# First block's attention: values by key tiles, later steps in the first pair, five early output tiles

## The chip, the cores and the metric

The kernel runs on one core of a Trainium2 chip. The core has TensorE (matrix products, with its own weight loads), VectorE, ScalarE and GpSimd (elementwise work), and SyncE, whose queue starts most DMAs. Each engine works through its own list of instructions in order and waits for others by semaphores. In the profile they are PE and PEld, DVE, ACT, POOL and SP. The metric is the device time of one execution in microseconds (us). Three runs of the kernel before took 1430.58, 1433.38 and 1433.93 us; the median is 1433.38.

## The reference

Two transformer blocks on 512 tokens of width 1024, in float32. The change touches the first one's mixer alone: attention of 16 heads of 64 with a forget gate, over 16 meta tokens and 512 real ones.

```python
def _fox_attend(q_blk, c_q, pos_q, k, v, c_k, pos_k):
    s = jnp.einsum('bhqd,bhkd->bhqk', q_blk, k).astype(jnp.float32) * (FOX_HEAD_DIM ** -0.5)
    s = s + (c_q[..., :, None] - c_k[..., None, :])
    s = jnp.where(pos_k[None, :] <= pos_q[:, None], s, -jnp.inf)
    p = jax.nn.softmax(s, axis=-1)
    return jnp.einsum('bhqk,bhkd->bhqd', p, v.astype(jnp.float32))

def fox_mixer(h, w_in, b_f, q_gain, k_gain, w_out):
    q, k, v, gate, f_logit = jnp.split(h @ w_in, [D, 2 * D, 3 * D, 4 * D], axis=-1)
    ...                                   # q, k: rms_norm over each head
    log_f = jax.nn.log_sigmoid(f_logit + b_f)
    c = jnp.cumsum(log_f, axis=1)
    ...                                   # _fox_attend in blocks of 128 queries
    o = o * jax.nn.sigmoid(gate)
    return o.astype(h.dtype) @ w_out
```

After it follow a gated feed-forward layer, and the second block with a chunked linear attention and a mixture of experts.

## The kernel before, in words

`fox` computes this mixer, and does two heads (a pair) at a time; there are eight pairs. All matrices are used in two parts, a rounded high one and the rest, so a product takes three matmuls per tile of 128 inputs.

**The order.** TensorE's main work is a list of projections, four per pair: queries (q), keys (k), values (v), gate (g). Each is made in eight parts (`project`, three matmuls of 512 columns per part, or six of 264). After each part `w.advance()` makes one step of a small planner (`Weave`): every piece of attention was put there with `at(delay, ...)`, counted in parts from the moment at which it was asked for. The delays are the table `F_V, Q_U, ...` at the head of the file. So the order of all instructions is fixed when the kernel is built, and pieces of one pair's attention stand between parts of the next pair's projections.

**The pieces.** `head_norm` takes a projection out of PSUM (L387), GpSimd makes its squares in two parts (`sqh` L391, `sql` L392), TensorE sums them over a head (L318, `sums`, due `Q_U` or `K_U` parts later), ScalarE and VectorE make the root of it (L220 to L228), VectorE scales (L401), and after `Q_H` or `K_H` parts the high and low copies for the scores are made (`hi`, `lo`; L428 to L450). For the first pair the forget gate's cumulated sum is made too (`forget_1` to `forget_3`, due `F_L`, and 2 and 4 parts after it).

`attend` puts down eight score blocks for the pair, four blocks of 128 queries for each of two heads (`scores`, every second part), each with its row maxima (L492), exponentials (L497) and scaling (L505). `F_F` parts after each comes `flip`: transposes of the probabilities on TensorE (L517) and their copy to `pt` by ScalarE (L519, the first five) or VectorE (L521). `values` (L529) multiplies them by the values, once per block of 128 queries, over the two to five key tiles that it sees: the blocks have 4, 6, 8 and 10 matmuls of 128 columns, the two heads in the two halves of the array's columns. `gated` and `gated_lo` then multiply by the gate into `ogh` and `ogl`.

In steady state the q sums stand three parts into the keys' projection, the k sums two parts into the values'. Three of the four `values` blocks stand ahead of the k sums.

**The end.** The output projection needs all pairs. So that TensorE has work during the last attention, three output tiles (`EARLY`) are computed without their last input tile first; then the planner is flushed, and the last input tile is added. The residual's input `h` is loaded by SP behind the weights that were asked for before. Transposes, sums and half a score block share the two PSUM slots `tp`; scores have `py`, projections `mm`.

Of the kernel before, what the change touches and what calls it, by code (L numbers as in the profile page):

```python
# [20 lines left out]
F32 = mybir.dt.float32  # L21
# [53 lines left out]

F_V, Q_U, Q_R, Q_H, Q_L, K_U, K_R, K_H, K_L, F_S, F_F, F_O, F_G, F_N, F_0, F_L = 6, 3, 2, 12, 1, 2, 2, 6, 2, 12, 8, 4, 12, 2, 5, 4

# [20 lines left out]
class Net:  # L98
# [142 lines left out]


    def fox(self):
        nc, tc, a = self.nc, self.tc, self.a
# [13 lines left out]

        fraw = wk.tile([P, KT, HEADS], F32, name="fraw")
        nc.scalar.dma_start(fraw, a["fw"])  # L260
# [21 lines left out]
        for i in range(NB):  # L282
            pt_off.append(pt_off[-1] + P * (i + 2))
        PW = pt_off[-1]
        pb = [sp.tile([P, PW], F32, name=f"pb{s}") for s in range(2)]
        for s in range(2):
# [7 lines left out]
        xl = sp.tile([P, KT, TM], F32R, name="xl")  # L294
        ss = sp.tile([P, TM], F32, name="ss")
        fhl = sp.tile([P, 2, KT, HEADS], F32R, name="fhl")
        self.split(fhl[:, 0], fhl[:, 1], fraw)
# [110 lines left out]
        def got_v(t, pv):  # L408
            v1 = wk.tile([P, TM], F32, name="v1", bufs=1)
            for p, o, n in pv:  # L410
                nc.vector.tensor_mul(v1[:, o:o + n], p, r1[:, o:o + n])

            def flip():
                vt = vts[t % 2]
                tp = pp.tile([P, T], F32, name="tp", bufs=2)
                for j in range(NB):
                    nc.tensor.transpose(tp[:, j * P:(j + 1) * P], v1[:, j * P:(j + 1) * P], self.ident)
                nc.scalar.activation(vt[:, 0:NB].rearrange("p j d -> p (j d)"), tp, AF.Copy)
                tp = pp.tile([P, T], F32, name="tp", bufs=2)
                nc.tensor.transpose(tp[:NM, :P], v1[:, T:TM], self.ident)  # L420
                nc.vector.tensor_copy(vt[:NM, NB], tp[:NM, :P])

            at(F_V, flip)

        def got_q(t, pq):
# [10 lines left out]

            head_norm(pq, self.qg, T, (hi, lo), Q_U, Q_R, Q_H, Q_L)

        def got_k(t, pk):
            def hi(kn):  # L440
                nc.scalar.activation(kd[A, 0], kn[A], AF.Copy)
                nc.scalar.activation(kd[B, 1], kn[B], AF.Copy)
                nc.scalar.dma_start(k2[HD:HD + 2, 0].bitcast(F32), nch[2 * t:2 * t + 1].bitcast(F32))
                nc.scalar.dma_start(k2[0:2, 1].bitcast(F32), nch[2 * t + 1:2 * t + 2].bitcast(F32))
                nc.scalar.activation(kd[B, 0], kn[A], AF.Copy)
                nc.scalar.activation(kd[A, 1], kn[B], AF.Copy)

# [3 lines left out]

            head_norm(pk, self.vec(V_KN), TM, (hi, lo), K_U, K_R, K_H, K_L)
            attend(t)
# [14 lines left out]
        def attend(t):  # L468
# [40 lines left out]
            def flip(i, s):  # L509
                if i == 0:  # L510
                    pts.append(wk.tile([P, PW], F32, name=f"pt{s}", bufs=1))
                for j0 in range(0, i + 2, 4):
                    n = min(4, i + 2 - j0) * P
                    c = pt_off[i] + j0 * P
                    tp = pp.tile([P, T], F32, name="tp", bufs=2)
                    for o in range(0, n, P):
                        nc.tensor.transpose(tp[:, o:o + P], pb[s][:, c + o:c + o + P], self.ident)  # L517
                    if F_E[2 * i + s]:
                        nc.scalar.activation(pts[s][:, c:c + n], tp[:, :n], AF.Copy)  # L519
                    else:  # L520
                        nc.vector.tensor_copy(pts[s][:, c:c + n], tp[:, :n])  # L521

            def values(i):
                if i == 0:
                    po.append(pp.tile([P, T], F32, name="plog", bufs=1))
                for j in range(i + 2):
                    c = pt_off[i] + j * P
                    for s in range(2):
                        nc.tensor.matmul(po[0][s * HD:(s + 1) * HD, i * P:(i + 1) * P],  # L529
                                         vt[:, j, s * HD:(s + 1) * HD], pts[s][:, c:c + P],  # L530
                                         start=(j == 0), stop=(j == i + 1), skip_group_check=True)

# [10 lines left out]
            for u in range(2 * NB):  # L543
                at(s0 + 2 * u, scores, u // 2, u % 2)
                at(s0 + F_F + 2 * u, flip, u // 2, u % 2)
            for i in range(NB):
                at(s0 + F_F + F_O + 4 * i + 2, values, i)
            at(s0 + F_F + F_O + 4 * NB, gated)
            at(s0 + F_F + F_O + 4 * NB + 2, gated_lo)

# [16 lines left out]
        self.w_at = 4 * PAIRS * KT  # L567
        EARLY = 3
        early = [mm() for _ in range(EARLY)]
        for p in early:  # L570
            for k in range(KT - 1):
# [14 lines left out]
        for m in range(KT):  # L586
            if m < EARLY:
                p = early[m]
# [973 lines left out]
def _layout(i):  # L1562
# [10 lines left out]
    wo = _tiles(f["fox_w_out"][0])  # L1573
    seq += [wo[:3, :7].reshape(-1, P, P), wo[:3, 7], *wo[3:]]
    wf, wo = _tiles(f["ffn_w_in"][0]), _tiles(f["ffn_w_out"][0])
# [53 lines left out]
```

## Time and profile before

| | |
|---|---|
| median of three runs | 1433.38 us |
| the profiled execution | 1431.87 us, span 1430.1 us |
| PE busy | 1355.8 us (95%), 8266 instructions |
| PEld busy | 1020.2 us (71%) |
| DVE, ACT, POOL busy | 739.3 (52%), 542.6 (38%), 118.9 us (8%) |

Busy shares are means over stages with different limits. The mixer takes about the first 340 us, and in it the engines other than PE are much busier than in the rest: in the page's 40 slices DVE shows 6 to 8 tenths in the first nine and 2 to 5 later. A row of the timeline gives the start, the time, the engine, the line, the operation, out<-in, the shape and how often; in brackets the engine's idle time before it, and what ended it. Rows of successive matmuls overlap, since each passes through a pipeline: their rate is read from their starts.

### The profile page before, as it was taken

How to read it: one execution, taken by the hardware profiler on the slowest of the kernel's cores; microseconds unless marked ns; L12 is line 12 of the kernel's file. 1: busy time of each engine (PE TensorE's matmuls, PEld its weight loads, DVE VectorE, ACT ScalarE, POOL GpSimd, SP SyncE). 2: the span in 40 equal slices, each digit the busy share in tenths (PEclk: the TensorE clock that was granted, in tenths of full speed). 3: DMA queues.
4: the chain of work that ended last, by engine and by line, in shares of the span. 5: the costliest groups of instructions: out<-in, count | busy, mean ns of one | idle time of the engine just before them, and what ended most of it. 6: DMA issues, size and time to landing. Idle time of an engine off the chain costs nothing.

```text
span 1430.1 us, 20194 instructions
## 1 busy us (share of the span) xinstructions
PE 1355.8 (95%) x8266; PEld 1020.2 (71%) x8266; DVE 739.3 (52%) x1321; ACT 542.6 (38%) x980; POOL 118.9 (8%) x111
## 2 busy tenths in 40 slices
PE   7899999999999999999999999999889999999995
PEld 5778888887888888888887888875556556556442
DVE  6778777785554433444456575542343432432333
ACT  6766776675433222323443444422111111111114
POOL 2101111111100000000322122000000000000001
PEclk9999999999999999999999999999989999999998
DMA  4111111113332222222221223698998999999995
GB/s 164 48 60 60 60 60 61 60 60 118 103 123 89 103 104 88 88 101 106 89 89 62 86 88 118 268 387 325 410 414 345 420 420 420 420 419 421 420 420 197
DMA packets 42495, 282.22 MB, mean 197 GB/s; under 512 B 4864, under 2 KB 5120, under 8 KB 9504
## 3 DMA queue, kind: packets, MB, share of 16 engines
q1 hardware_dynamic: 41616, 280.05, 49.3%
q8 instruction: 66, 1.08, 0.3%
q10 hardware_dynamic: 784, 0.85, 0.2%
q14 instruction: 29, 0.24, 0.0%
HBM read 278.72 MB, written 2.10 MB: 196 GB/s over the span
## 4 chain that ended last, share of the span: by engine, by line
PE 68%; DMA 19%; DVE 7%; ACT 3%; POOL 1%; issue 1%; SPq 0%; ACTq 0%; POOLq 0%; DVEq 0%
PE mm L205 22%; DMA wring<-in_w_dram 12%; PE mm L331 10%; PE py L205 8%; PE tp L205 8%; PE tp L1269 4%; PE mm L1359 3%; DMA v<-in_w_dram 3%; DMA wraw<-in_w_dram 3%; PE mm L773 2%; PE py L1303 2%; DMA whl<-in_w_dram 1%; PE plog L529 1%; POOL sql L392 1%; PE tp L517 1%; DVE whl L178 1%
## 5 line engine op out<-in xcount | busy, mean ns | idle before, releaser
L178 DVE TENSOR_TENSOR whl<-wraw,whl 128x1024 fp32r<-128x1024 f32 x138 | 180.8, 1310 | 100.2 <-ACT whl L168 100.0
L331 PE MATMUL mm<-xh,whl 128*128 128x264 f32 (+1 forms) x736 | 183.3, 333 | 2.2 <-ACT whl L168 2.1
L168 ACT ACTIVATE whl<-wraw 128x1024 fp32r<-128x1024 f32 x138 | 144.5, 1050 | 105.0 <-PE mm L205 44.3
L205 PE MATMUL mm<-xh,whl 128*128 128x512 f32 x544 | 175.9, 397 | 0.0
L331 PEld LDWEIGHTS mm<-xh,whl 128*128 128x128 f32 x736 | 120.6, 190 | 17.6 <-issue 3.4
L1269 PEld LDWEIGHTS tp<-h,xt 128*128 128x128 f32 x1024 | 115.9, 192 | 6.9 <-issue 2.5
L205 PEld LDWEIGHTS mm<-xh,whl 128*128 128x128 f32 x544 | 102.2, 188 | 23.1 <-issue 2.3
L1269 PE MATMUL tp<-h,xt 128*128 128x128 f32 x1024 | 118.4, 276 | 0.2 <-DVE h L1260 0.2
L205 PE MATMUL mm<-xl,whl 128*128 128x512 f32 x272 | 106.0, 390 | 0.0
L331 PE MATMUL mm<-xl,whl 128*128 128x264 f32 (+1 forms) x368 | 100.1, 325 | 0.0
L1359 PE MATMUL mm<-wring,h 128*32 128x512 f32 x664 | 96.1, 595 | 3.4 <-ACT h L1272 2.0
L1308 DVE SCALAR_TENSOR_TENSOR h<-py,sv,h 128x512 fp32r<-128x512 f32 (+1 forms) x33 | 24.1, 734 | 143.3 <-ACT h L1305 143.3
L205 PE MATMUL mm<-ogh,whl 128*128 128x512 f32 x256 | 83.6, 396 | 1.5 <-ACT ogh L536 1.5
L1272 ACT ACTIVATE h<-tp,vecs 128x128 f32<-128x128 f32 x128 | 36.5, 368 | 105.1 <-PE tp L1269 105.1
L1370 ACT ACTIVATE tmp<-mm,sv 128x256 f32<-128x256 f32 x16 | 7.6, 473 | 181.0 <-PE mm L1359 165.9
L1289 DVE TENSOR_TENSOR acc<-acc,mm 128x512 f32<-128x512 f32 (+1 forms) x120 | 73.8, 673 | 1.3 <-PE mm L1288 1.0
L1287 PE MATMUL mm<-h,ss 128*128 128x512 f32 (+1 forms) x128 | 61.8, 484 | 9.2 <-DVE acc L1289 5.1
L205 PE MATMUL py<-xh,whl 128*128 128x512 f32 x208 | 65.8, 391 | 0.0
L205 PE MATMUL tp<-xh,whl 128*128 128x512 f32 x208 | 65.2, 389 | 0.0
L331 PEld LDWEIGHTS mm<-xl,whl 128*128 128x128 f32 x368 | 62.2, 191 | 3.3
L616 POOL TENSOR_TENSOR ss<-ss,sq 128x512 f32<-128x512 f32 x21 | 29.1, 1401 | 403.0 <-ACT sq L612 403.0
L205 PEld LDWEIGHTS mm<-xl,whl 128*128 128x128 f32 x272 | 51.1, 188 | 11.5 <-issue 1.4
(420 smaller groups left out, 2539.2 us busy)
## 6 DMA issues: line engine op xcount, KB each, us to landing
wring<-in_w_dram SPq DMA_DIRECT2D x120, 1024.0 KB, 19.8
wraw<-in_wd_dram SPq DMA_DIRECT2D x69, 1024.0 KB, 4.8
whl<-in_w_dram SPq DMA_DIRECT2D x27, 1024.0 KB, 16.8
v<-in_w_dram SPq DMA_DIRECT2D x20, 1024.0 KB, 18.0
wraw<-in_w_dram SPq DMA_DIRECT2D x18, 1024.0 KB, 19.8
h<-in_xT_dram SPq DMA_DIRECT2D x8, 256.0 KB, 5.6
acc<-in_w_dram SPq DMA_DIRECT2D x2, 1024.0 KB
wring<-in_w_dram SPq DMA_DIRECT2D x4, 512.0 KB, 17.0
```

Source lines behind the costliest of these rows:

```text
L168: self.nc.scalar.activation(hl[:, 0], raw, AF.Copy)
L178: self.nc.vector.tensor_sub(hl[:, 1], raw, hl[:, 0].bitcast(F32))
L205: self.nc.tensor.matmul(out, w, x[:, first + k], start=(at + k == 0 and e == 0), stop=(at + k == of - 1 and e == 2))
L331: nc.tensor.matmul(p[:rows, :m], w[:, wi, k], xx[:, k, o:o + m], start=(n == 0), stop=(n == 3 * KT - 1))
L616: nc.gpsimd.tensor_add(ss, ss, sq)
L773: nc.tensor.matmul(pv[b], x[:, k, bs], w2[:, wi, k % 2], start=(k == 0 and e == 0), stop=(k == KT - 1 and e == 2))
L1269: nc.tensor.matmul(p[:, k], self.xt[:, b, (k0 + k) * P:(k0 + k + 1) * P], oh[:, 1, b], start=(b + k == 0), stop=(b == NB - 1), skip_group_ ...
L1272: nc.scalar.activation(xs[:, k0 + k], p[:, k], AF.Copy, scale=self.vec(V_FN2, k0 + k))
L1287: nc.tensor.matmul(pc, gt[:, b * P:(b + 1) * P], yh[:, hs], start=True, stop=False)
L1289: nc.vector.tensor_add(acc[b][:, hs], acc[b][:, hs] if q else self.xt[:, b, hs], pc)
L1303: nc.tensor.matmul(out, hT[:, e, js], w, start=(e == 0), stop=(e == 1))
L1359: nc.tensor.matmul(ps[32 * j:32 * j + 32], xs[:, kind * 4 + k, 32 * j:32 * j + 32], self.ring[kind, 4 * q + j][:, k * T:(k + 1) * T], star ...
```

## The change

1. `values` goes by key tiles: for each of the five key tiles and each head one matmul over all queries that see that tile (512, 512, 384, 256 and 128 columns), where it was one block of queries over its key tiles. `pt` is laid out by key tile for it, with `flip`'s copies writing up to four runs of 128. All of a pair's `values` now come after its last `flip`, from `F_O` parts on, one key tile per part; `gated` and `gated_lo` come 2 and 4 parts behind.
2. In the first pair the keys' steps come later (`K_0`), the flip of the values too (`F_V0`), the attention starts 9 instead of 5 parts later than in other pairs (`F_0`), the forget gate 6 instead of 4 (`F_L`); the second pair's query copies come at 14 instead of 12 (`Q_H1`).
3. `EARLY` is 5 instead of 3; the last two of these tiles take `py` slots.
4. In `got_k` all four key copies precede the two small DMAs into `k2`.
5. `fraw`, `ss` and `fhl` take buffers of names that are used later.

```diff
-F_V, Q_U, Q_R, Q_H, Q_L, K_U, K_R, K_H, K_L, F_S, F_F, F_O, F_G, F_N, F_0, F_L = 6, 3, 2, 12, 1, 2, 2, 6, 2, 12, 8, 4, 12, 2, 5, 4
+F_V, Q_U, Q_R, Q_H, Q_L, K_U, K_R, K_H, K_L, F_S, F_F, F_O, F_G, F_N, F_0, F_L = 6, 3, 2, 12, 1, 2, 2, 6, 2, 12, 8, 3, 12, 2, 9, 6
+
+F_V0, K_0, Q_H1 = 14, (9, 2, 13, 2), 14
...
-        fraw = wk.tile([P, KT, HEADS], F32, name="fraw")
+        fraw = wk.tile([P, KT, HEADS], F32, name="sqh", bufs=2)
...
-        ss = sp.tile([P, TM], F32, name="ss")
-        fhl = sp.tile([P, 2, KT, HEADS], F32R, name="fhl")
+        ss = wk.tile([P, TM], F32, name="sql", bufs=2)
+        fhl = wk.tile([P, 2, KT, HEADS], F32R, name="v1")
...
-            at(F_V, flip)
+            at(F_V if t else F_V0, flip)
...
-            head_norm(pq, self.qg, T, (hi, lo), Q_U, Q_R, Q_H, Q_L)
+            head_norm(pq, self.qg, T, (hi, lo), Q_U, Q_R, Q_H1 if t == 1 else Q_H, Q_L)
...
                 nc.scalar.activation(kd[B, 1], kn[B], AF.Copy)
+                nc.scalar.activation(kd[B, 0], kn[A], AF.Copy)
+                nc.scalar.activation(kd[A, 1], kn[B], AF.Copy)
                 nc.scalar.dma_start(k2[HD:HD + 2, 0].bitcast(F32), nch[2 * t:2 * t + 1].bitcast(F32))
                 nc.scalar.dma_start(k2[0:2, 1].bitcast(F32), nch[2 * t + 1:2 * t + 2].bitcast(F32))
-                nc.scalar.activation(kd[B, 0], kn[A], AF.Copy)
-                nc.scalar.activation(kd[A, 1], kn[B], AF.Copy)
...
-            head_norm(pk, self.vec(V_KN), TM, (hi, lo), K_U, K_R, K_H, K_L)
+            head_norm(pk, self.vec(V_KN), TM, (hi, lo), *((K_U, K_R, K_H, K_L) if t else K_0))
...
             def flip(i, s):
                 if i == 0:
-                    pts.append(wk.tile([P, PW], F32, name=f"pt{s}", bufs=1))
+                    pts.append(wk.tile([P, NB + 1, T], F32, name=f"pt{s}", bufs=1))
...
+                    dst = pts[s][:, j0:j0 + n, i * P:(i + 1) * P]
...
-            def values(i):
-                if i == 0:
+                        nc.vector.tensor_copy(dst, tp[:, :n])
+
+            def values(j):
+                if j == 0:
                     po.append(pp.tile([P, T], F32, name="plog", bufs=1))
-                for j in range(i + 2):
-                    c = pt_off[i] + j * P
-                    for s in range(2):
-                        nc.tensor.matmul(po[0][s * HD:(s + 1) * HD, i * P:(i + 1) * P],
-                                         vt[:, j, s * HD:(s + 1) * HD], pts[s][:, c:c + P],
-                                         start=(j == 0), stop=(j == i + 1), skip_group_check=True)
+                for s in range(2):
+                    nc.tensor.matmul(po[0][s * HD:(s + 1) * HD, first_q[j]:], vt[:, j, s * HD:(s + 1) * HD],
+                                     pts[s][:, j, first_q[j]:], start=(j == 0), stop=(j == NB),
+                                     skip_group_check=True)
...
-            for i in range(NB):
-                at(s0 + F_F + F_O + 4 * i + 2, values, i)
-            at(s0 + F_F + F_O + 4 * NB, gated)
-            at(s0 + F_F + F_O + 4 * NB + 2, gated_lo)
+            o0 = s0 + F_F + 4 * NB - 2 + F_O
+            for j in range(NB + 1):
+                at(o0 + j, values, j)
+            at(o0 + NB + 2, gated)
+            at(o0 + NB + 4, gated_lo)
...
-        EARLY = 3
-        early = [mm() for _ in range(EARLY)]
-        for p in early:
+        early = []
+        for n in range(self.EARLY):
+            p = mm() if n < 3 else f_bank()
+            early.append(p)
```

On TensorE, in the fifth pair's projections: the last rows of the fourth pair's attention and the fifth's keys' sums. `pb` are probabilities, `plog` the output of `values`, `sqh` and `sql` the squares. Before:

```order
L517 MATMUL tp<-ident,pb_129 128x128 x4
L529 MATMUL plog<-pt_1801,vt_139 64x128
L529 MATMUL plog<-pt_1821,vt_139 64x128
...
L331 MATMUL mm<-xh,whl 128x264 x2
L517 MATMUL tp<-ident,pb_129 128x128 x5
L529 MATMUL plog<-pt_1801,vt_139 64x128
L529 MATMUL plog<-pt_1821,vt_139 64x128
...
L318 MATMUL tp<-sqh,hones 128x264
L318 MATMUL tp<-sql,hones 128x264
```

And of the kernel after, the same place:

```order
L524 MATMUL tp<-ident,pb_129 128x128 x5
L325 MATMUL tp<-sqh,hones 128x264
L325 MATMUL tp<-sql,hones 128x264
...
L535 MATMUL plog<-pt_1747,vt_139 64x512
L535 MATMUL plog<-pt_1767,vt_139 64x512
L338 MATMUL mm<-xh,whl 128x264 x2
L338 MATMUL mm<-xl,whl 128x264 x2
L338 MATMUL mm<-xh,whl 128x264 x2
L535 MATMUL plog<-pt_1747,vt_139 64x512
L535 MATMUL plog<-pt_1767,vt_139 64x512
```

The `values` rows between and behind the transposes are gone from there; the keys' sums follow the last transposes at once, and all values come behind them, one key tile after each part.

On ScalarE, where the second pair's query and key copies stand (`qs`, `q` and `kd`, `k`), near the end of the first pair's probabilities. Before:

```order
L519 ACTIVATE pt_624<-tp 128x512
L428 ACTIVATE qs<-q_559 64x512
L429 ACTIVATE qs<-q_559 64x512
L430 ACTIVATE q_122<-q_559 64x512
L431 ACTIVATE q_122<-q_559 64x512
L441 ACTIVATE kd<-q_681 64x528
L442 ACTIVATE kd<-q_681 64x528
L443 DMA k_123<-nch 2x1x528
L444 DMA k_123<-nch 2x1x528
L445 ACTIVATE kd<-q_681 64x528
```

After:

```order
L435 ACTIVATE qs<-q_543 64x512
L436 ACTIVATE qs<-q_543 64x512
L437 ACTIVATE q_122<-q_543 64x512
L438 ACTIVATE q_122<-q_543 64x512
L448 ACTIVATE kd<-q_653 64x528
L449 ACTIVATE kd<-q_653 64x528
L450 ACTIVATE kd<-q_653 64x528
L451 ACTIVATE kd<-q_653 64x528
L452 DMA k_123<-nch 2x1x528
L453 DMA k_123<-nch 2x1x528
L527 ACTIVATE pt_662<-tp 128x4x128
```

The copy of the fifth transposed block to `pt` stood ahead of the query copies and now stands behind the key copies and the DMAs.

## Rows read from the trace of the kernel before

**Rows 1.** Windows, one pair: stretch, us, engines' busy time, PEclk, DMA share, GB/s.

```profile
173.45:189.90 16.45, 15.81 (x137) 14.10 (x136) 13.91 (x28) 11.67 (x24) 5.58 (x4) 1.00 0.05 9
189.90:210.18 20.28, 20.28 (x133) 16.95 (x132) 15.43 (x33) 14.13 (x30) 0.00 (x0) 1.00 0.26 98
```

**Rows 2.** Timeline of PE in these two stretches (start, us, what).

```profile
177.10 0.66 PE L529 MATMUL plog<-pt,vt 128*64 128x128 f32 x8
177.69 0.51 PE L331 MATMUL mm<-xh,whl 128*128 128x264 f32 x2
...
180.26 0.66 PE L517 MATMUL tp<-ident,pb 128*128 128x128 f32 x4 [0.38 <-ACT pb L497]
...
187.78 1.09 PE L529 MATMUL plog<-pt,vt 128*64 128x128 f32 x16
...
189.43 0.39 PE L318 MATMUL tp<-sql,hones 128*128 128x264 f32 x1
...
192.57 0.41 PE L331 MATMUL mm<-xh,whl 128*128 128x264 f32 x2
192.91 1.31 PE L529 MATMUL plog<-pt,vt 128*64 128x128 f32 x20
194.15 0.51 PE L331 MATMUL mm<-xh,whl 128*128 128x264 f32 x2
```

**Rows 3.** Timeline of DVE in the first of the two.

```profile
173.65 0.69 DVE L387 TENSOR_TENSOR q<-mm,r 128x512 f32<-128x512 f32 x1 [0.28 <-PE mm L331]
...
175.59 1.48 DVE L505 TENSOR_SCALAR pb<-pb,mx 128x400 f32<-128x400 f32 x1
...
178.47 0.41 DVE L492 TENSOR_REDUCE mx<-tp 128x1 f32<-128x264 f32 x1
...
180.81 0.69 DVE L222 TENSOR_SCALAR rs_x<-tp 128x512 f32<-128x512 f32 x1 [0.94 <-ACT rr L220]
...
185.21 0.77 DVE L387 TENSOR_TENSOR q<-mm,r 128x264 f32<-128x264 f32 x2
```

**Rows 4.** Timeline of ACT there.

```profile
179.64 0.47 ACT L497 ACTIVATE pb<-tp,mx 128x264 f32<-128x264 f32 x1
```

**Rows 5.** Timeline of POOL there.

```profile
187.21 2.17 POOL L392 TENSOR_TENSOR sql<-sq,sqh 128x528 fp32r<-128x528 f32 x1
```

**Rows 6.** Timeline of PE in the experts' stage, four column groups.

```profile
1204.25 0.60 PE L1359 MATMUL mm<-whl,h 128*32 128x512 f32 x3
...
1204.67 0.60 PE L1359 MATMUL mm<-whl,h 128*32 128x512 f32 x3
```

**Rows 7.** Waits of PE, 26 to 80 us: who for whom, us in total, times, longest.

```profile
PE tp L417 <- DVE v L411: 3.1, 1, 3.1
PE tp L318 <- POOL sql L392: 2.1, 2, 1.1
PE tp L318 <- ACT pb L497: 1.6, 1, 1.6
```

**Rows 8.** Windows in the first pair.

```profile
46.50:52.00 5.50, 5.47 (x16) 4.38 (x17) 3.38 (x5) 2.45 (x5) 0.00 (x0) 0.50 0.01 2
70.00:76.00 6.00, 4.12 (x36) 3.51 (x34) 4.18 (x9) 4.64 (x14) 1.33 (x1) 1.00 0.33 112
```

**Rows 9.** Timeline of PE in the first pair.

```profile
36.38 0.39 PE L318 MATMUL tp<-sql,hones 128*128 128x264 f32 x1 [0.99 <-POOL sql L392]
```

**Rows 10.** Timeline of ACT in the first pair.

```profile
50.48 0.64 ACT L445 ACTIVATE kd<-q 64x528 fp32r<-64x528 f32 x1 [3.01 <-DVE k L450]
51.13 0.64 ACT L446 ACTIVATE kd<-q 64x528 fp32r<-64x528 f32 x1
```

**Rows 11.** Timeline of PE at the mixer's end.

```profile
339.25 0.50 PE L205 MATMUL mm<-ogh,whl 128*128 128x512 f32 x1 [1.48 <-ACT ogh L536]
...
339.98 0.50 PE L205 MATMUL mm<-ogl,whl 128*128 128x512 f32 x1 [0.22 <-DVE ogl L540]
```

**Rows 12.** The page's part 6, DMA issues: count, KB each, us to landing.

```profile
wraw<-in_wd_dram SPq DMA_DIRECT2D x69, 1024.0 KB, 4.8
```

More of the change, by code (lines that the diff above doesn't have):

```diff
@@ L240, in split @@
             nc.vector.scalar_tensor_tensor(lo, src, scale, hi.bitcast(F32), op0=OP.mult, op1=OP.subtract)
+    EARLY = 5
     def fox(self):
@@ L284, in fox @@
         PW = pt_off[-1]
+        first_q = [max(j - 1, 0) * P for j in range(NB + 1)]
         pb = [sp.tile([P, PW], F32, name=f"pb{s}") for s in range(2)]
@@ L510, in flip @@
                 if i == 0:
-                    pts.append(wk.tile([P, PW], F32, name=f"pt{s}", bufs=1))
+                    pts.append(wk.tile([P, NB + 1, T], F32, name=f"pt{s}", bufs=1))
                 for j0 in range(0, i + 2, 4):
-                    n = min(4, i + 2 - j0) * P
+                    n = min(4, i + 2 - j0)
                     c = pt_off[i] + j0 * P
-                    tp = pp.tile([P, T], F32, name="tp", bufs=2)
-                    for o in range(0, n, P):
-                        nc.tensor.transpose(tp[:, o:o + P], pb[s][:, c + o:c + o + P], self.ident)
+                    tp = pp.tile([P, 4, P], F32, name="tp", bufs=2)
+                    for o in range(n):
+                        nc.tensor.transpose(tp[:, o], pb[s][:, c + o * P:c + (o + 1) * P], self.ident)
+                    dst = pts[s][:, j0:j0 + n, i * P:(i + 1) * P]
                     if F_E[2 * i + s]:
-                        nc.scalar.activation(pts[s][:, c:c + n], tp[:, :n], AF.Copy)
+                        nc.scalar.activation(dst, tp[:, :n], AF.Copy)
                     else:
-                        nc.vector.tensor_copy(pts[s][:, c:c + n], tp[:, :n])
-            def values(i):
-                if i == 0:
+                        nc.vector.tensor_copy(dst, tp[:, :n])
+            def values(j):
+                if j == 0:
                     po.append(pp.tile([P, T], F32, name="plog", bufs=1))
-                for j in range(i + 2):
-                    c = pt_off[i] + j * P
-                    for s in range(2):
-                        nc.tensor.matmul(po[0][s * HD:(s + 1) * HD, i * P:(i + 1) * P],
-                                         vt[:, j, s * HD:(s + 1) * HD], pts[s][:, c:c + P],
-                                         start=(j == 0), stop=(j == i + 1), skip_group_check=True)
+                for s in range(2):
+                    nc.tensor.matmul(po[0][s * HD:(s + 1) * HD, first_q[j]:], vt[:, j, s * HD:(s + 1) * HD],
+                                     pts[s][:, j, first_q[j]:], start=(j == 0), stop=(j == NB),
+                                     skip_group_check=True)
             def gated():
@@ L586, in fox @@
         for m in range(KT):
-            if m < EARLY:
+            if m < self.EARLY:
                 p = early[m]
@@ L1573, in _layout @@
     wo = _tiles(f["fox_w_out"][0])
-    seq += [wo[:3, :7].reshape(-1, P, P), wo[:3, 7], *wo[3:]]
+    e = Net.EARLY
+    seq += [wo[:e, :7].reshape(-1, P, P), wo[:e, 7], *wo[e:]]
     wf, wo = _tiles(f["ffn_w_in"][0]), _tiles(f["ffn_w_out"][0])
```

## The prediction

> **What bounds the kernel now.** The change touches only the first block's attention, about the first 340 of 1430 us, so I read the windows of one pair of heads first, then each engine's timeline in it. In steady state a pair takes 36.73 us, and it falls into two stretches of different kind [rows 1]. Stretch A, 16.45 us, runs from the end of the next pair's query projection to the sums of squares of its keys; there TensorE has holes. In stretch B, 20.28 us, TensorE is busy for all 20.28 us: it sets the pace alone. The reader is to see this contrast, because the change moves TensorE work from A to B.
>
> What sets the pace in A? I followed it through the other engines [rows 2 to 5]. The queries' end lets VectorE start at 173.65. Its scaling of a probability block then takes 1.48 us; the maxima of the eighth score block come only at 178.47, though TensorE had left those scores before 177.10. ScalarE's exponential of them runs at 179.64, the logarithm for the queries comes behind it, VectorE waits for that until 180.81 and reaches the keys' scaling at 185.21. GpSimd's second square pass starts at 187.21 and takes 2.17 us, and TensorE starts the last sums at 189.43. Nowhere in this chain does an engine wait for a values matmul. TensorE's transposes at 180.26 themselves wait for ScalarE [rows 2]. So A is a chain of VectorE, ScalarE and GpSimd, into whose waits three of the four values blocks (8, 12 and 16 records at 177.10, at 182.75 by the same pattern, and at 187.78) are put as filler. The fourth, at 192.91, lies in B.
>
> **The change, part by part.**
>
> *Values by key tiles.* Columns first: before, 28 matmuls of 128 columns; after, 10 of 512, 512, 384, 256 and 128 (two heads each). Both are 3584, so nothing is saved in streaming. The records show two per matmul. From the starts of the 8-record block and its successor (0.59 us) and of the 20-record block and its successor (1.24 us) [rows 2], a record costs (1.24 - 0.59) / 12 = 0.054 us. The block at 192.91 follows two matmuls begun at 192.57; 528 columns at 2.4 GHz are 0.22 us, so the block costs 194.15 - 192.79 = 1.36 us, of which 20 x 0.054 = 1.08 is streaming and 0.28 is the price of entering and leaving. Are 512 columns run beside each other as well as 128? No such two-head matmul is in this trace; the nearest is the expert stage, where four column groups of 512 columns take 0.42 us per four records [rows 6], which is two passes of 512 columns at 2.4 GHz for all four at once. I take the same rate. All five blocks then cost 56 x 0.054 + 5 x 0.28 = 4.43 us, where the four cost 3.03 + 1.12 = 4.15. The bounds are 3.03 (no block price) and 7.5 (the two heads one after the other).
>
> The Trainium skill, in TensorEngine Tiling (Array Packing), section Instruction Overhead, speaks against this: each matmul has an overhead of about 60 cycles, so 36 fewer records would save an estimated 36 x 25 ns = 0.9 us a pair. The records' 0.054 us for 128 columns leaves no room for it (128 columns at 2.4 GHz are 0.053). By the rule each of eight pairs would take 0.9 us less, and the sum below would come to about 1442.
>
> *Their place.* The rows in the order of TensorE show that all five blocks now stand behind the last sums of the keys, in B. A loses 36 x 0.054 + 3 x 0.28 = 2.79 us of TensorE work. If the chain sets A, A stays at 16.45 us: I followed it above, and the order of VectorE's instructions in A is unchanged. B, which TensorE sets, gets 4.43 - 1.36 = 3.07 us more. So **a pair takes 3.07 us longer**; if A shrank by the whole 2.79, it would be 0.28. I take 3.07, the row-by-row chain. It holds for the attention of pairs 1 to 6, which lies beside projections of pairs 2 to 7: 6 x 3.07 = 18.4 us. For the first and the last pair I count the fifth block alone: 2 x 0.28 = 0.6 us. The gating and its two halves come later too; the projection behind them covers that, since nothing reads them before the output projection.
>
> *The first pair.* It removes waits of TensorE: 3.1 us for the values' scaling, 2.1 and 1.6 us among others [rows 7], and after the first of these 5.50 us at a granted clock of 0.50, 1.2 GHz [rows 8], of which half, 2.75 us, is lost. That is 9.5 us at best. It brings waits. (a) The keys' sums move from 36.38 [rows 9] to behind four parts of the gate, near 39.2 by counting the parts ahead at 0.70 to 0.73 us each (three matmuls of 512 columns, or six of 264, with the gaps between them); the copies of the keys ended 15.4 us after the sums, 3.0 of them blocked by the two small DMAs that now come behind them [rows 10]. With four query copies of about 0.64 us now ahead of the key copies, the first scores can start at about 39.2 + 15.4 - 3.0 + 4 x 0.64 = 54, or 1 us sooner, as the last copies serve the second head only: 53. TensorE has work, twelve more parts and the transposes of the values, until about 49, so it waits some 4 us, and again the clock may fall for 2.75 us. (b) ScalarE now copies the fifth of the eight transposed probability blocks (the order's second place) behind four query and four key copies, 8 x 0.64 = 5.1 us; two parts of projection, 1.4 us, and two pieces of attention cover some 2.1 of it, so about 3 us show in a later transpose that needs the slot. Removed 9.5, brought about 4 + 2.75 + 3 = 9.8: **I take 0**, with -9.5 (none of the new waits) and +5 (old ones at 60 to 75 us stay) as ends.
>
> *Five output tiles early.* The work is the same, 42 matmuls of 512 columns come earlier. They cover the last pair's gating, at which TensorE waits 1.48 + 0.22 = **1.7 us** now [rows 11]; that goes. What would be late next are the residual's loads, which stand behind one weight load more on SP's queue: that is hidden by 14 more steps of TensorE work; without the cover it is at most one weight load, 4.8 us [rows 12].
>
> *Buffers.* The forget weights and the sum of squares share buffers with later tiles; their readers are long done when those are first written: nothing either way. The key copies before the DMAs: later pairs reach their scores 3 us later, which covers it; at worst 2 x 0.64 us a pair.
>
> **Sum.** The profiled execution took 1431.87 us (span 1430.1), 1.5 below the median of the runs, which I do not add. 1431.87 + 18.4 + 0.6 + 0 - 1.7 = **1449.2 us**.
>
> **Rivals.**
> 1. *TensorE sets A after all* (not slower). If VectorE's chain would move up when TensorE arrives earlier, each pair pays 0.28: 1431.87 + 6 x 0.28 + 0.6 - 1.7 = 1432.5 us; with the first pair's best end it is 1423. For it: TensorE is 15.81 of 16.45 us busy in A. Against: 180.26 and 189.43 wait for ScalarE and GpSimd already. It decides where the keys' end at 185.21 moves up against the queries' end.
> 2. *The clock falls in the longer holes.* The wait of 0.38 us before 180.26 would grow by the first block's 0.7, the one before 189.43 by the third block's 1.1, in every pair. If that sends the clock to 0.50 as the 3.1 us wait did, six times 2.75 us come on top: about 1466 us. Against: the wait of 1.6 us in the first pair lies in a stretch at 1.00 [rows 8].
> 3. *The two heads' matmuls run one after the other at 512 columns*, so the change doesn't do what it says: 3.03 us more in eight pairs, 1449 + 24 = 1473 us. Against: [rows 6].
>
> **How the numbers follow.** Forecast 0.75, rival 1 0.15, rival 2 0.06, rival 3 0.04. The forecast's own range, by the first pair's ends, is 1439 to 1455. The range is 1432 to 1460: it leaves out the lower part of rival 1 and rivals 2 and 3. About 0.3%, 4.3 us, can be told from no change. Slower: forecast, rivals 2 and 3, less what the first pair's best end and an error of mine in the chain could take: 0.80. No change: most of rival 1 and a little of the forecast, 0.13. Faster: rival 1 with a good first pair, 0.07.
>
> **What would show it.** Right: a pair's period near 39.8 us; from the queries' end to the keys' sums still about 16.4, with TensorE's busy time there down by some 2.8; a wait of TensorE for GpSimd's second square pass longer by about 1.1 us in every pair; B near 23.4 and fully busy; a block of four 512-column records about 0.87 us plus 0.28; no wait for the gating at the end. Wrong: a period near 37 us (rival 1), a granted clock below 1.00 between 90 and 310 us (rival 2), blocks of 1.7 us (rival 3), or first scores of the first pair well before 53 us.

## Result and profile after

| | runs | median | lowest to highest |
|---|---|---|---|
| before | 4 | 1432.37 us | 1430.58 to 1433.93 |
| after | 4 | 1453.77 us | 1452.15 to 1456.64 |

The table has one more run of the kernel before (1431.36 us) than the three that were known ahead of the prediction. The ratio is 1.0149, with a 95% interval of 1.0136 to 1.0162: the change makes the kernel 21.4 us slower. The profiled execution took 1456.64 us, the slowest of the four. Its page (its span, then each engine's busy time):

```profile
span 1454.9 us, 19626 instructions
...
PE 1367.5 (94%) x7978; PEld 1006.6 (69%) x7978; DVE 738.7 (51%) x1321; ACT 543.8 (37%) x980; POOL 119.8 (8%) x111
```

TensorE is busy 11.7 us longer though it runs 288 matmul records fewer (36 per pair), so some 13 us of the 24.8 us of span are idle time. Where? First the two stretches of one pair, as in [rows 1], here from the queries' end to the end of the keys' sums and from there to the next queries' end; columns are span, then PE, PEld, DVE, ACT, POOL, PEclk, DMA share, GB/s:

```profile
183.69:199.94 16.25, 13.60 (x101) 12.21 (x100) 13.82 (x28) 11.66 (x24) 5.58 (x4) 1.00 0.04 6
199.94:223.59 23.65, 23.65 (x134) 16.95 (x132) 15.54 (x33) 14.35 (x30) 0.00 (x0) 1.00 0.23 87
```

Stretch A is 16.25 us long against 16.45, though TensorE works 13.60 us in it instead of 15.81. Stretch B has become 23.65 us instead of 20.28, and TensorE is busy in all of it. The clock is 1.00 in both. So the reader sees 2.2 us of TensorE's work leave A, and A stay as it was.

TensorE's own timeline shows what took the place of the values in A, against [rows 2]:

```profile
190.49 0.66 PE L524 MATMUL tp<-ident,pb 128*128 128x128 f32 x4 [0.75 <-ACT pb L504]
...
195.39 0.33 PE L524 MATMUL tp<-ident,pb 128*128 128x128 f32 x1 [0.43 <-DVE pt L529]
...
198.99 0.36 PE L325 MATMUL tp<-sqh,hones 128*128 128x264 f32 x1 [1.10 <-DVE pt L529]
199.47 0.39 PE L325 MATMUL tp<-sql,hones 128*128 128x264 f32 x1
...
201.87 0.40 PE L338 MATMUL mm<-xh,whl 128*128 128x264 f32 x2
202.21 1.08 PE L535 MATMUL plog<-pt,vt 128*64 128x512 f32 x4
203.22 0.51 PE L338 MATMUL mm<-xh,whl 128*128 128x264 f32 x2
```

The wait for exponentials has grown from 0.38 to 0.75 us (190.49), a wait of 0.43 for a copy is new (195.39), and so is one of 1.10 before the keys' sums (198.99). A block of values is the row at 202.21. It lies between the end of the two matmuls begun at 201.87 (528 columns, 0.22 us) and 203.22, so it takes 1.13 us; [rows 2] had 1.36 for the largest of the old blocks.

The release at 198.99 is VectorE's. Its timeline:

```profile
196.72 1.52 DVE L180 TENSOR_TENSOR whl<-wraw,whl 128x1024 fp32r<-128x1024 f32 x1
198.16 0.88 DVE L529 COPY pt<-tp 128x512 f32<-128x512 f32 x2
```

Its last copies to `pt`, which free a slot `tp` for the sums, stand behind a weight split of 1.52 us. But they are not what ends A. The second sums start only at 199.47, 0.48 us behind the first, and this is 0.05 us after GpSimd's second square pass ends (197.24 + 2.18 = 199.42):

```profile
197.24 2.18 POOL L399 TENSOR_TENSOR sql<-sq,sqh 128x528 fp32r<-128x528 f32 x1
```

In the kernel before it was the same: that pass ends at 187.21 + 2.17 = 189.38, and the second sums start at 189.43 [rows 2, 5]. So in both traces A's end follows GpSimd's pass, and an earlier copy alone would not have brought the second sums forward; no run tried it.

How the difference adds up is read from GpSimd's first square pass of each pair's queries, which marks the start of a period. After (third, fourth and eighth pair):

```profile
104.26 1.04 POOL L398 TENSOR_TENSOR sqh<-q 128x512 fp32r<-128x512 f32 x1 [36.49 <-ACT ogh L542]
...
144.76 1.04 POOL L398 TENSOR_TENSOR sqh<-q 128x512 fp32r<-128x512 f32 x1 [25.14 <-DVE q L394]
...
304.34 1.04 POOL L398 TENSOR_TENSOR sqh<-q 128x512 fp32r<-128x512 f32 x1 [25.16 <-DVE q L394]
```

Before (third and eighth):

```profile
100.97 1.04 POOL L391 TENSOR_TENSOR sqh<-q 128x512 fp32r<-128x512 f32 x1 [29.53 <-DVE q L387]
...
284.67 1.04 POOL L391 TENSOR_TENSOR sqh<-q 128x512 fp32r<-128x512 f32 x1 [21.81 <-DVE q L387]
```

The third pair starts 104.26 - 100.97 = 3.29 us later. The eighth starts 304.34 - 284.67 = 19.67 later, so five periods cost 16.38, the first of them 3.8 and the others 3.15 each. A product of the feed-forward layer that stood at 391.78 stands at 414.02: 22.24 later, 2.57 more. The rest of this profile's 24.8 us is lost in the experts' stage (last section).

### The profile page after: what moved, and what is told of

The parts are those of the page before. It is cut to its first block, busy times and chain, and to the rows that moved or that the text cites. A ratio compares the mean times of both kernels' runs of the same rounds, so it can differ in the third digit from the quotient of the medians.

```text
span 1454.9 us, 19626 instructions
## 1 busy us (share of the span) xinstructions
PE 1367.5 (94%) x7978; PEld 1006.6 (69%) x7978; DVE 738.7 (51%) x1321; ACT 543.8 (37%) x980; POOL 119.8 (8%) x111
## 4 chain that ended last, share of the span: by engine, by line
PE 78%; DVE 7%; ACT 7%; DMA 3%; POOL 2%; issue 2%; ACTq 0%; SPq 0%; POOLq 0%; DVEq 0%
PE mm L207 19%; PE mm L338 8%; PE py L207 8%; PE tp L1277 7%; PE tp L207 7%; PE mm L1367 7%; PE py L1311 4%; DMA wring<-in_w_dram 3%; PE mm L781 2%; PE plog L535 2%; PE mm L1295 2%; PE tp L1288 2%; PE mm L1296 2%; POOL sql L399 1%; DVE whl L180 1%
## 5 line engine op out<-in xcount | busy, mean ns | idle before, releaser
L338 PE MATMUL mm<-xh,whl 128*128 128x264 f32 (+1 forms) x736 | 190.6, 337 | 2.4 <-ACT whl L170 1.5
L207 PE MATMUL mm<-ogh,whl 128*128 128x512 f32 x224 | 73.6, 395 | 0.0
## 6 DMA issues: line engine op xcount, KB each, us to landing
whl<-in_w_dram SPq DMA_DIRECT2D x27, 1024.0 KB, 11.7
```

Source lines behind the costliest of these rows:

```text
L207: self.nc.tensor.matmul(out, w, x[:, first + k], start=(at + k == 0 and e == 0), stop=(at + k == of - 1 and e == 2))
L338: nc.tensor.matmul(p[:rows, :m], w[:, wi, k], xx[:, k, o:o + m], start=(n == 0), stop=(n == 3 * KT - 1))
```

## Experiments

All times are against the kernel before on the same chip (1432.4 to 1433.3 us in the four sets). "A period" is the row of the stretch between two such square passes. The edits are shown in part: `...` marks lines left out, and the lines of the table of delays are shortened to the names that bear on the run.

**1. Values by key tiles alone.**

```diff
-F_O, F_0, F_L = 4, 5, 4
+F_O, F_0, F_L = 3, 5, 4
-            def values(i):
+            def values(j):
...
+            for j in range(NB + 1):
+                at(o0 + j, values, j)
```

> The kernel before with part 1 of the change alone: values by key tiles, all behind the pair's last transposes. My theory (TensorE work leaves a stretch that other engines pace and is put into one that TensorE paces): the period of a pair 36.73 becomes 39.9 us, as in the changed kernel, so 6 x 3.15 = 18.9 us for pairs 2 to 7, and some 3 us more where the first pair's values leave its holes too: about +20 to +22 us against the kernel before. Rival (the first pair's moved steps and the five early tiles carry a good part of the 21 us): under +15 us.

**2. The old blocks at the new place.**

```diff
-                at(s0 + F_F + F_O + 4 * i + 2, values, i)
-            at(s0 + F_F + F_O + 4 * NB, gated)
+            o0 = s0 + F_F + 4 * NB - 2 + F_O
...
+                at(o0 + i, values, i)
+            at(o0 + NB + 2, gated)
```

> The kernel before with its own values, by query blocks of 128 columns (28 matmuls of two heads' halves), put where the changed kernel has them: all behind the last transposes, one block after each part; the gating as late as in the change. Theory (the place costs): B gets 36 records x 0.054 + 3 x 0.28 = 2.79 us per pair, the period is 39.5, and the kernel is slower by 17 to 19 us. Rival (the form costs: matmuls of 512 columns of two heads, output written over all queries): the form is the old one, so within 4 us of the kernel before.

Measured: by key tiles 1456.55 us, ratio 1.0167 (1.0152 to 1.0182); old blocks late 1450.24 us, 1.0123 (1.0105 to 1.0141). The second is 17.8 us slower, as its theory has it. The first is 24.1 us slower, 2 more than its theory's 20 to 22: at the feed-forward product named above its trace is 20.96 behind (that of old blocks late 17.56), and most of the rest is lost in the experts' stage. One period of the kernel before, of old blocks late, of key tiles alone and of the changed kernel:

```profile
174.42:211.17 36.75, 36.11 (x270) 31.05 (x269) 29.35 (x62) 25.82 (x51) 5.58 (x5) 1.00 0.16 58
```

```profile
181.82:221.37 39.55, 36.91 (x270) 31.23 (x269) 29.36 (x62) 26.02 (x51) 5.58 (x5) 1.00 0.15 54
```

```profile
182.29:222.14 39.85, 37.22 (x234) 29.17 (x233) 29.33 (x62) 26.03 (x51) 5.57 (x4) 1.00 0.14 54
```

```profile
184.66:224.56 39.90, 37.25 (x234) 29.16 (x233) 29.36 (x62) 26.00 (x51) 5.59 (x5) 1.00 0.15 54
```

Span less busy time of TensorE is its idle time: 0.64 us before, 2.64, 2.63 and 2.65 in the others. Moving the old blocks makes 2.80 of the 3.15 us; the form by key tiles adds 0.30, and that is busy time. Of the 2.80, 2.00 are idle time and 0.80 busy time with the same matmuls: with the old blocks late, TensorE works 2.20 us less in A (13.61 instead of 15.81), and B is 3.02 longer (23.30). Why the same blocks cost more in B was not taken apart. The theory holds, the rival of the form falls: the place carries nine tenths of what a period grows by. The 1.0167 rules out that other parts of the change carry it.

**3. Five early output tiles alone.**

```diff
-        EARLY = 3
+    EARLY = 5
...
+            p = mm() if n < 3 else f_bank()
```

> The kernel before with five early output tiles alone. Theory: the wait for the gating at the mixer's end, 1.48 + 0.22 us, is covered: 1.7 us faster. Rival (the loads of the residual come later behind one more weight load, and the wait only moves there): no change or slower by up to 4.8 us.

Measured: 1432.43 us, ratio 0.9999 (0.9991 to 1.0008). The waits for the gating are gone from the trace, but nothing is gained that can be measured. VectorE's first and last addition to the residual, before:

```profile
340.75 0.69 DVE L592 TENSOR_TENSOR h<-h,mm 128x512 f32<-128x512 f32 x1 [0.82 <-PE mm L205]
...
369.34 0.69 DVE L592 TENSOR_TENSOR h<-h,mm 128x512 f32<-128x512 f32 x1 [0.95 <-PE mm L205]
```

and with five early tiles:

```profile
347.58 0.69 DVE L595 TENSOR_TENSOR h<-h,mm 128x512 f32<-128x512 f32 x1 [0.35 <-PE mm L205]
...
369.45 0.67 DVE L595 TENSOR_TENSOR h<-h,mm 128x512 f32<-128x512 f32 x1
```

The additions start 6.8 us later and end at the same time, since VectorE takes over 2.1 us for each of them with what it does for the norm, and 4.4 for the last three. Counted from the eighth pair's square pass, TensorE comes to the feed-forward layer 2.1 us earlier, and gives back 1.1 of it in waits there, one of them for the norm's sum on GpSimd:

```profile
372.88 1.12 PE L645 MATMUL plog<-ss,ones 128*128 128x512 f32 x2 [0.43 <-POOL ss L619]
```

At the product of the feed-forward layer 0.9 us is left. In this execution more than that, 1.5 us, is lost at 774 us, in the second block: behind a wait of 0.91 us the clock is at 0.50 (1.2 GHz), while in the kernel before, behind the same wait of 0.92 us, it stays at 1.00.

```profile
770.68 0.46 PE L851 MATMUL tp<-qe,ke 128*128 128x128 f32 x2 [0.91 <-DVE ke L841]
```

```profile
774.00:776.00 2.00, 2.00 (x7) 1.64 (x6) 0.45 (x1) 0.49 (x1) 0.00 (x0) 0.50 0.00 0
```

The times neither show the 0.9 us nor rule it out (their interval is 1.3 us faster to 1.1 slower). The rival was right that a part of the wait moves, and wrong on to what: to VectorE's additions and the norm, not to a load.

**4. The first pair's steps and the key copies alone.**

```diff
+F_V0, K_0, Q_H1 = 14, (9, 2, 13, 2), 14
...
-F_0, F_L = 5, 4
+F_0, F_L = 9, 6
```

> The kernel before with the first pair's later steps and the key copies ahead of the two DMAs, values as before. Theory (what it removes, 9.5 us, comes back as two waits of 3.5 us for ScalarE's copies, each followed by a stretch at half the clock): the net is within 2 us of nothing. Rival (the waits after the change come from the values' new place): 6 to 9 us faster.

Measured: 1430.32 us, ratio 0.9985 (0.9973 to 0.9997), 2.1 us faster: the net is near nothing, as the theory has it, but just beyond its 2 us, and far from the rival's 6 to 9. From the first square pass to the feed-forward product its trace takes 362.19 us, that of the kernel before 362.17, so the 2.1 us do not show in the mixer; where they come from is open. Its timeline of TensorE where the fifth transposed block is waited for:

```profile
77.25 0.88 PE L531 MATMUL plog<-pt,vt 128*64 128x128 f32 x12
...
81.43 0.66 PE L519 MATMUL tp<-ident,pb 128*128 128x128 f32 x4 [1.70 <-ACT pt L521]
83.05 0.33 PE L519 MATMUL tp<-ident,pb 128*128 128x128 f32 x1 [0.97 <-DVE pt L523]
```

The waits are 1.70 and 0.97 us, and a block of values stands at 77.25. In the changed kernel the same place has no values, and the waits are 3.47 and 0.51; the first scores' wait is the same in both. TensorE after:

```profile
52.32 0.33 PE L493 MATMUL py<-kd,qs 128*128 128x144 f32 x1 [3.50 <-ACT kd L450]
...
81.89 1.12 PE L524 MATMUL tp<-ident,pb 128*128 128x128 f32 x4 [3.47 <-ACT pt L527]
```

and windows behind these waits:

```profile
54.00:56.00 2.00, 2.00 (x10) 1.89 (x10) 2.00 (x3) 2.00 (x6) 1.47 (x2) 0.50 0.94 393
82.00:84.00 2.00, 1.49 (x7) 1.02 (x7) 2.00 (x3) 0.92 (x1) 0.00 (x0) 0.50 0.00 0
84.00:86.00 2.00, 2.00 (x7) 1.71 (x7) 0.63 (x3) 0.47 (x2) 0.00 (x0) 0.50 0.00 0
86.00:88.00 2.00, 2.00 (x10) 1.59 (x9) 0.00 (x0) 0.00 (x0) 0.00 (x0) 0.55 0.00 0
88.00:90.00 2.00, 1.61 (x12) 1.36 (x11) 1.50 (x6) 0.84 (x3) 0.00 (x0) 1.00 0.00 0
```

The clock stands at 0.50 at 54 to 56 us and again from 82 to 86, and returns only at 88. So the values' new place makes the first pair's new wait worse: the third pair starts 1.59 us late with key tiles alone, 0.49 early with the first pair's steps alone, and 3.29 late with both. Counted from the first square pass of each trace, so that differences of the start-up drop out, these are 2.29, -0.07 and 3.25 us: most of it comes with the values' place alone, in run 1, whose clock is at 1.00 from 60 to 106 us, and about 1.0 us from the two together.

**5. The changed kernel with that copy on VectorE.**

```diff
-                    if F_E[2 * i + s]:
+                    if F_E[2 * i + s] and (t or 2 * i + s < 4):
```

> The changed kernel, with one copy of the first pair given to VectorE: the fifth transposed block (f4), which stands behind eight copies on ScalarE, so that the next transposes wait 3.47 us for it and then run at half the clock until 87. Theory: that wait and the clock's fall go together, 3.5 + 2.7 = 6 us faster than the changed kernel (about 1447.5, 15 us above the kernel before); a part of it comes back if VectorE is late itself. Rival (the half clock there has another cause than the wait): 3.5 us at most.

Measured: 1454.69 us, ratio 1.0151 (1.0137 to 1.0165); nothing gained on 1453.77. The wait has changed engines, in two pieces:

```profile
79.76 0.66 PE L524 MATMUL tp<-ident,pb 128*128 128x128 f32 x4 [1.26 <-DVE pt L529]
83.72 0.47 PE L524 MATMUL tp<-ident,pb 128*128 128x128 f32 x1 [3.31 <-DVE pt L529]
```

```profile
78.00:82.00 4.00, 1.16 (x7) 0.49 (x5) 3.87 (x10) 3.88 (x7) 0.00 (x0) 1.00 0.01 2
82.00:86.00 4.00, 2.27 (x8) 1.92 (x9) 2.84 (x5) 1.02 (x3) 0.00 (x0) 0.55 0.00 0
```

From 78 to 82 us VectorE is busy 3.87 and ScalarE 3.88 of 4 us. Which of them makes the copy doesn't matter: both are full, and TensorE has run ahead of both. My theory on this wait falls.

**6. The changed kernel with the keys' sums two parts later.**

```diff
-K_U, K_R, K_H, K_L = 2, 2, 6, 2
+K_U, K_R, K_H, K_L = 4, 2, 7, 2
```

> The changed kernel with the keys' sums of pairs 2 to 8 two parts of projection later (their root and copies one to two later too). Theory: TensorE fills its wait of 1.1 us before the sums with these parts, and nothing else is late: the period falls from 39.9 to about 38.8, some 7 us faster than the changed kernel (1447). Rival (the chain of VectorE and ScalarE as a whole sets stretch A, and the wait moves to the next place that needs them): within 2 us of the changed kernel.

Measured: 1445.79 us, ratio 1.0082 (1.0068 to 1.0096), 8.0 us faster than the changed kernel. The wait before the sums is gone, and a period is 1.41 us shorter:

```profile
182.19:220.68 38.49, 37.04 (x234) 29.16 (x233) 29.36 (x62) 26.03 (x51) 5.61 (x5) 1.00 0.16 56
```

The waits for exponentials and copies are as they were (1.45 us idle are left). So TensorE can fill a wait of A with projection, if the piece that waits is asked for later: A is held by the fixed order, in which TensorE stands and waits for a chain of pieces, and not by an engine that is full: VectorE, the busiest of the others, works 13.82 of A's 16.25 us in the changed kernel. The rival falls.

**7. The first pair in another order, values as before.**

```diff
+F_V0, K_0, Q_H1 = 14, (6, 2, 11, 2), 14
...
+                    if F_E[2 * i + s] and (t or 2 * i + s < 4):
```

> The kernel before with the first pair's later steps as in the run of these alone, but the keys' sums 6 instead of 9 parts later and their copies at 11 instead of 13, beside the forget gate's chain instead of behind it, and the fifth transposed block copied by VectorE. Theory (the two waits for ScalarE's copies, each with a stretch at half the clock, ate what the first pair gained): both go or shrink, 6 to 10 us faster than the kernel before, 1423 to 1426. Rival (other waits of the first pair take their place): within 3 us of the kernel before.

Measured: 1432.97 us, ratio 1.0002 (0.9992 to 1.0011). The first scores wait 1.63 instead of 3.50 us, the transposes later 2.98:

```profile
50.72 0.34 PE L488 MATMUL py<-kd,qs 128*128 128x144 f32 x1 [1.63 <-DVE sg L459]
...
84.58 0.33 PE L519 MATMUL tp<-ident,pb 128*128 128x128 f32 x1 [2.98 <-DVE pt L523]
```

The clock falls behind both (0.54 to 0.60 from 54 to 62 us, 0.69 from 86 to 90). The rival was right: another order only moves these waits.

**8. Fewer values in A.**

```diff
-                for j in range(i + 2):
+                n = i + 2 if i == 3 else 1
+                for j in range(n):
```

> The kernel before without 24 of the 56 values' matmuls of a pair, all of them in the three blocks that stand in stretch A: each of these blocks takes only its first key tile (so this part of the attention's sum is left out). Theory (in A they fill TensorE's waits, and A is set by the other engines): A stays at 16.2 to 16.45 us and the whole within 0 to 2 us of the kernel before, plus 1.3 us each in the first and last pair at best. Rival (TensorE sets A): 24 x 0.054 = 1.3 us per pair, 10.4 us faster in eight pairs.

Measured: 1429.40 us, ratio 0.9974 (0.9965 to 0.9984), 3.5 us faster. In its trace the third pair starts 1.5 us sooner, and each period is 0.2 shorter. Stretch A and one period:

```profile
171.57:187.81 16.24, 14.74 (x114) 12.86 (x113) 13.81 (x28) 11.69 (x24) 5.57 (x4) 1.00 0.04 9
172.54:209.09 36.55, 35.05 (x246) 29.80 (x245) 29.26 (x62) 25.84 (x51) 5.57 (x5) 1.00 0.17 59
```

TensorE has 1.07 us less to do in A than in [rows 1], and A ends 0.21 us sooner. This is the cleanest view of it: four fifths of the work taken from A give nothing. The theory holds, with A at 16.24 us; the 3.5 us lie within the 2 us, and 1.3 each for the first and the last pair, that it allowed. The rival's 10.4 us fall.

**9 and 10. The kernel before with later sums and later transposes; the same with the first pair's steps.**

```diff
-K_U, K_R, K_H, K_L, F_S, F_F, F_O = 2, 2, 6, 2, 12, 8, 4
+K_U, K_R, K_H, K_L, F_S, F_F, F_O = 4, 2, 7, 2, 12, 9, 3
```

> The kernel before with its values where they were, the keys' sums of pairs 2 to 8 two parts later and the transposes one part later after their scores. Theory (A is set by waits that one or two parts of projection can fill, here one of 0.38 us a pair that shows and little beside it): 0.4 to 0.6 us per pair, 2 to 4 us faster than the kernel before. Rival (with its values in A as filler, the kernel before has nothing left to gain there): within 1.5 us.

> The same and the first pair's later steps with the key copies ahead of the DMAs: a version that could beat both kernels. Theory: the two gains add, 2 to 4 and 2 us, 1427 to 1429. Rival (transposes one part later push the first pair's second wait further out): no gain over the other.

Measured: 1451.81 us, ratio 1.0133 (1.0115 to 1.0151), and 1447.15 us, 1.0094 (1.0078 to 1.0109). Neither theory nor rival: both are far slower, with a period of 39.27. Two of the new waits of the first:

```profile
186.90 0.47 PE L318 MATMUL tp<-sqh,hones 128*128 128x512 f32 x1 [1.34 <-ACT pb L497]
...
207.69 0.33 PE L488 MATMUL py<-k,q 128*128 128x144 f32 x1 [0.64 <-DVE k L449]
```

The queries' sums wait 1.34 us for exponentials that read half a score block from the slot they need. The likely reason is that the transposes now come in odd parts and take the two slots in another turn; the turn itself was not traced. The scores wait 0.64 for the low key copies. The first pair's steps are worth more here, 4.7 us, than alone.

**11. The changed kernel with later sums and transposes two parts later.**

```diff
-K_U, K_R, K_H, K_L, F_S, F_F = 2, 2, 6, 2, 12, 8
+K_U, K_R, K_H, K_L, F_S, F_F = 4, 2, 7, 2, 12, 10
```

> The changed kernel with the keys' sums two parts later and the transposes two parts later after their scores. Theory: of the 1.36 us a pair that TensorE still waited with later sums alone (0.75 for exponentials, 0.43 and 0.18 for copies) most goes, the period falls from 38.49 to 37.2 to 37.8, and the kernel comes to 1438 to 1442; it stays behind the kernel before, since each pair has five blocks to enter and leave instead of four. Rival (VectorE's and ScalarE's chain holds the period): 38.4 and 1446.

Measured: 1446.42 us, ratio 1.0089 (1.0074 to 1.0103). It is no better than run 6, as the rival says; a period is 38.89, 0.40 longer than there:

```profile
181.83:220.72 38.89, 36.86 (x234) 28.75 (x233) 29.54 (x62) 25.89 (x51) 4.98 (x4) 1.00 0.15 55
```

Later transposes did not fill the waits for exponentials that later sums had left. What sets them was not taken apart further.

**12. The kernel before with the first pair's steps and later sums alone.**

```diff
-K_U, K_R, K_H, K_L = 2, 2, 6, 2
+K_U, K_R, K_H, K_L = 4, 2, 7, 2
```

> The kernel before with the first pair's later steps, the key copies ahead of the DMAs, and the keys' sums of pairs 2 to 8 two parts later; transposes as they were. The two runs with later sums and transposes one part later were 14 to 18 us slower than the kernel before, with a new wait of 1.3 us a pair of the queries' sums for exponentials that read the slot they need, and one of 0.6 for the low key copies. Theory (the transposes' odd step, which changes the turn of the two shared slots, made the first and most of it): here 36.4 to 37.0 us per pair, 1427 to 1432, no more than 1 us off the run with the first pair's steps alone. Rival (the later sums made it): 38.5 us per pair or more, 1441 and up.

Measured: 1434.61 us, ratio 1.0014 (1.0004 to 1.0024). A period is 37.18, 0.43 longer than before, where the theory had 37.0 at most and the rival 38.5; the time, 4.3 us above run 4's, misses the theory's 1427 to 1432:

```profile
174.84:212.02 37.18, 36.06 (x270) 31.09 (x269) 29.27 (x62) 25.93 (x51) 5.58 (x5) 1.00 0.17 58
```

Run 10, which differs from this run in the transposes' step alone, has 39.27. So the odd step made 2.1 of the 2.5 us per period of runs 9 and 10. The later sums cost the rest: the scores wait for the low key copies, six times in this view of TensorE's waits (total, times, longest):

```profile
PE py L490 <- DVE k L451: 3.9, 6, 0.7
```

Of all versions that compute the whole attention, that of run 4 is the fastest: 1430.32 us, 2.1 below the kernel before.

## Why the prediction was right

Slower was right, and for the reason given; 1449.2 was 4.6 us short of the median of 1453.77, inside the range.

- *A is set by the other engines.* Right, in the order as it stands. A lost 2.2 us of TensorE's work (2.8 forecast) and kept its length but for 0.20; run 8 shows the same by taking work away. The chain ends at GpSimd's second square pass, as I had it: the second sums start 0.05 us behind it in both kernels. The new wait is as long as forecast (1.10 for 1.1), but it comes ahead of the first sums and VectorE's copy, which I had not followed, releases it. Run 6 adds what I had not asked: with the sums later in the order, TensorE fills this wait with projection.
- *The period.* 39.90 for 39.8. Its two terms, place and form, were 2.79 and 0.28; runs 2 and 1 measured 2.80 and 0.30. That 2.79 fits so well is in part luck: in run 2 A lost 2.20 and shrank by 0.20, and B grew by 3.02. Runs 2 and 1 also bear on the rule of the Trainium skill, in TensorEngine Tiling (Array Packing), section Instruction Overhead, read as about 60 cycles on top of every matmul: with the place held fixed, 36 fewer records did not save the estimated 0.9 us a pair but cost 0.30. The trace does not agree with that reading for these 128-column matmuls.
- *B fully busy.* Right: 23.65 for 23.4.
- *The first pair* is the term that was mis-sized: 0, and 0.28 for its fifth block, where the third pair starts 3.29 us late. The moved steps alone are worth -2.1 us in the times and nothing in the mixer's trace, inside the ends, and the first scores start at 52.32 after a wait of 3.50 (53 and 4 forecast). But I priced the first pair's values as if they already stood in the open. They were filler there too, and with key tiles alone their new place costs 2.29 us. With the moved steps they are missed a second time, in the hole that the new wait for the fifth copy makes: the wait came out 3.47 (3 forecast), where run 4, with values ahead of it, waits 1.70. Behind it the clock fell a second time, which I had counted once. Together this is about 1.0 us more. Nor is the wait due to that copy's place in ScalarE's row, as I had it: run 5 moved the copy, and the wait stayed.
- *Five early tiles.* Wrong: -1.7 forecast, 0.0 (-1.3 to +1.1) measured. I named the residual's loads as next in line and did not count VectorE's additions and the norm, which end when they did before: in run 3's trace 0.9 us is left at the feed-forward product. In the changed kernel, against run 1 with its three tiles, the way from the eighth square pass to that product is 1.2 us shorter.
- *Sum.* Against 17.3 forecast the mixer's 22.2 has 3.0 more in the first pair, 1.0 more in five periods, and 0.9 more behind them, where the early tiles gave less than 1.7.
- *Rivals.* TensorE setting A (rival 1) falls with run 8, the clock in the longer holes (rival 2) with a granted clock of 1.00 from 90 to 310 us, the two heads one after the other (rival 3) with blocks of 1.13 us.

## What to carry to other kernels

Before moving work out of a stretch, ask what sets that stretch: if TensorE's work there stands in its waits for other engines, it is nearly free (four fifths of it in run 8), and moved to where TensorE paces everything it costs its full length, in its old form (run 2) as in a new one (run 1). A wait at a fixed place in an order written out by hand can be filled by asking for the waiting piece later (run 6), but only where nothing reads its result soon (run 12). Such a shift can cost more than it gains where it changes the steps at which pieces take shared slots (runs 9 and 10 against run 12).

## What the runs showed of the hardware beyond that

Whether the granted clock falls after a wait differs between executions of nearly the same work. In the experts' stage TensorE of the changed kernel and of run 5 waits 1.69 us for the same addition:

```profile
1031.58 0.50 PE L1295 MATMUL mm<-h,ss 128*128 128x512 f32 x1 [1.69 <-DVE acc L1297]
```

```profile
1031.85 0.50 PE L1295 MATMUL mm<-h,ss 128*128 128x512 f32 x1 [1.69 <-DVE acc L1297]
```

and in the ten microseconds around it the clock is 0.66 in the first and 1.00 in the second:

```profile
1030.00:1040.00 10.00, 7.88 (x32) 3.46 (x36) 6.29 (x13) 0.38 (x1) 0.00 (x0) 0.66 0.97 406
```

```profile
1030.00:1040.00 10.00, 7.78 (x51) 3.42 (x51) 7.12 (x16) 1.51 (x3) 0.00 (x0) 1.00 1.00 415
```

The first one lost 2.5 us there against the second. Run 3 lost 1.5 us in the same way at 774 us. The 2.5 us would be most of the 2.9 us by which the profiled execution of the changed kernel lies above its median; the other executions have no trace to show it. Such differences are the reason for reading a difference of a few microseconds from a stretch and not from the span. The waits of 3.1 to 3.5 us in the first pair were each followed by a fall in the four traces read there (before, after, runs 4 and 5). What decides it for the shorter waits stays open.
